# An adding DMA in a seven-product scheme: one weight sum moves from VectorE to a DMA, and ten groups get a fourth seven-product pair

## The chip, the cores and the metric

The kernel runs on one core of a Trainium2 chip. The metric is the time of one execution on the device in microseconds; runs of a kernel are compared by their medians.

## The reference

Two layers of a decoder trunk over 256 tokens of width 2048, in float32. Layer 0 mixes with sliding-window attention beside an mLSTM, layer 1 with forgetting attention; after each mixer stands a SwiGLU feed-forward part, and this is what the change touches:

```python
def swiglu(xn, w_gate, w_up, w_down):
    return (jax.nn.silu(xn @ w_gate) * (xn @ w_up)) @ w_down
...
h = h + swiglu(rms_norm(h, norm_ffn[layer]), w_gate[layer], w_up[layer], w_down[layer])
```

`w_gate` and `w_up` are 2048 x 5632, `w_down` is 5632 x 2048. The gain of the norm is put into the split activations (`xh`, `xl`), its scale `r` is applied after the products.

## The kernel before

Every float32 operand is split in two float32r parts, `hi` (a cast on ScalarE, lines 187 and 356) and `lo` (what is left, a subtraction on VectorE, lines 188 and 357), and a product is three matmuls (`three`, lines 532 to 534): hi x hi, hi x lo, lo x hi. The weights come from memory in tiles of 256 rows x 512 columns (512 KB, `load_raw`, line 134, issued by SP), and each tile's parts go into one of eight slots (`slot`, tiles `hi` and `lo`) that rotate: a slot is written again when TensorE has read what was in it.

A layer's 5632 hidden columns are eleven groups of 512. The groups come in three parts (0 to 2, 3 to 6, 7 to 10); behind each part stands the down product of its rows. `ffn` calls `pair_group` for each gate/up group, with the two weight matrices (gate columns, up columns), and for each pair of 512-column blocks of the down product. `pair_group` walks along the inner dimension in eight steps of 256 (six where a part has three groups), two row blocks of 128 at a time. Such a step is called a pair. With the two token blocks and the two matrices, a pair is a 2 x 2 by 2 x 2 block product, once for each column of 512. A *plain* pair does it in eight products, 24 matmuls, from two weight tiles split as they are. A *mixed* pair does it in seven products, 21 matmuls, in the manner of Strassen and Winograd: it needs sums of activation blocks (`sums`, made once and kept in `sx` and `sd`, `x4` for pair 7) and four sums of weight blocks, made for each pair on VectorE:

```python
ra, rb = (load_raw(w, k0, c0, NB, fp, W_RAWS if halves else RAWS, raws) for w, c0 in mats)
```

`ra` is the gate tile of the pair (rows k0, k0+1) and `rb` the up tile (for a down pair, the first and the second column block). Lines 607 to 610 make the four differences, 512 elements a partition each, into a tile `t4` and in place into `ra`; then `t4` and `ra` are split. `order` says which pairs are mixed: `ORDER` has three of eight, `HEAVY` four; a group takes `HEAVY` where its number is in `DENSE`, which is empty, so all groups take `ORDER`. At a group's end `combine` (lines 553 to 570) puts the products together, and silu and the product of gate and up follow (lines 665 to 672). Mixed pairs outside the feed-forward part take other buffers (`halves` given).

Raw tiles of mixed pairs rotate through `RAWS` = 4 buffers; a load waits until the tile four loads earlier was read for the last time. Raw tiles of plain pairs have four buffers of their own.

The program is written pair by pair, but a scheduler orders the instructions of each engine at build time. Each engine then works through its own queue in that order, and waits where an operand or a buffer is not ready. SP's queue holds the loads, GpSimd's the DMAs that it issues itself.

Of the kernel before, what the change touches and what calls it, by code (L numbers as in the profile page):

```python
# [7 lines left out]
F32 = mybir.dt.float32  # L8
# [4 lines left out]
ALU = mybir.AluOpType  # L13
# [4 lines left out]
P = 128  # L18
# [5 lines left out]
NB = 512  # L24
CK = 2
# [10 lines left out]
ORDER = ((0, 0), (1, 1), (0, 2), (1, 3), (0, 4), (1, 5), (0, 6), (0, 7))  # L36
HEAVY = ((1, 1), (0, 0), (1, 3), (0, 2), (1, 5), (0, 4), (1, 7), (0, 6))
FOURTH = 7
DENSE = ()
DOWN = {  # L40
    6: ((0, 0), (1, 1), (0, 2), (1, 3), (0, 4), (0, 5)),
    8: ((0, 0), (1, 1), (0, 2), (1, 3), (0, 4), (1, 5), (0, 6), (0, 7)),
# [9 lines left out]
W_RAWS = 4  # L52
LATER = (6, 10, 3, 5)
LATER_DOWN = (5, 6)
RAWS = 4
P_JOIN = 4
COLD = 9
TURNED = (0,)
# [17 lines left out]
def trunk(  # L76
# [19 lines left out]
    nc = tc.nc  # L96
# [31 lines left out]
    def load_raw(w, k0, c0, n, pool=wr, bufs=4, raws=None):  # L128
        if raws:
            raw = raws.pop(0)  # L130
            raws.append(raw)
        else:
            raw = pool.tile([P, CK, NB], F32, tag="raw", name="raw", bufs=bufs)
        loaded[0] = nc.sync.dma_start(
            raw[:, :, 0:n], w[k0 * P : (k0 + CK) * P, c0 : c0 + n].rearrange("(k p) n -> p k n", p=P)
        )
        return raw
# [46 lines left out]
    def split_chunk(raw, n):  # L184
        hi, lo = slot()
        for k in (slice(0, 1), slice(1, CK)) if any(raw is f for f in fine) else (slice(0, CK),):
            latest[0] = nc.scalar.copy(hi[:, k, 0:n], raw[:, k, 0:n])  # L187
            nc.vector.tensor_tensor(  # L188
                out=lo[:, k, 0:n], in0=raw[:, k, 0:n], in1=hi[:, k, 0:n].bitcast(F32), op=ALU.subtract
            )  # L190
        return hi, lo
# [71 lines left out]
    def sums_of(pool, sh, sl, copies, full=None, tags=("tmp", "tmp"), bufs=None, box=None, x4=None):  # L263
        if box is not None:
            full, s = box[:, 0:4, :].rearrange("p (i t) q -> p i t q", i=2), box[:, 4:8, :]
            copies(full.rearrange("p i t q -> p i (t q)"))
        elif full is None:
            full = pool.tile([P, 2, NT, P], F32, tag=tags[0], name="full", bufs=bufs)
            copies(full.rearrange("p i t q -> p i (t q)"))
        if box is None:  # L270
            s = pool.tile([P, 4, P], F32, tag=tags[1], name="s4", bufs=bufs)
        nc.vector.tensor_tensor(out=s[:, 0, :], in0=full[:, 0, 1, :], in1=full[:, 1, 1, :], op=ALU.add)
        nc.vector.tensor_tensor(out=s[:, 1, :], in0=s[:, 0, :], in1=full[:, 0, 0, :], op=ALU.subtract)
        nc.vector.tensor_tensor(out=s[:, 2, :], in0=full[:, 0, 0, :], in1=full[:, 0, 1, :], op=ALU.subtract)
        nc.vector.tensor_tensor(out=s[:, 3, :], in0=full[:, 1, 0, :], in1=s[:, 1, :], op=ALU.subtract)
        if x4 is None:
            split_plain(sh, sl, s)
        else:
            split_plain(sh, sl, s[:, 0:3, :])
            split_plain(x4[:, 0, :], x4[:, 1, :], s[:, 3, :])  # L280
# [258 lines left out]
    def pair_group(fp, par, lhs, sums, mats, order, todo=(), halves=None, inner=None, raws=None):  # L539
        plain = [[bank(par, "acc") for _ in range(NT)] for _ in range(2)]  # L540
        begun = set()

        def fresh(*at):
            known = at in begun
            begun.add(at)
            return not known

        todo = list(todo)
        prods = None
        kinds = [kind for kind, _ in order]  # L550
        t0, t1 = slice(0, P), slice(P, 2 * P)

        def combine(prods):
            c = fp.tile([P, 4, NB], F32, tag="c", name="c", bufs=1)
            nc.scalar.copy(c[:, 0, :], prods[0])
            if halves is None:
                nc.vector.tensor_tensor(out=c[:, 1, :], in0=prods[3], in1=c[:, 0, :], op=ALU.add)
                nc.vector.tensor_tensor(out=c[:, 2, :], in0=prods[2], in1=c[:, 1, :], op=ALU.add)
                nc.vector.tensor_tensor(
                    out=c[:, 1:4:2, :],  # L560
                    in0=prods[1].rearrange("p (a n) -> p a n", a=1).broadcast_to([P, 2, NB]),
                    in1=c[:, 1:3, :],
                    op=ALU.add,
                )
                return c
            nc.vector.tensor_tensor(out=c[:, 2, :], in0=prods[3], in1=c[:, 0, :], op=ALU.add)
            nc.vector.tensor_tensor(out=c[:, 1, :], in0=prods[2], in1=c[:, 2, :], op=ALU.add)
            nc.vector.tensor_tensor(out=c[:, 3, :], in0=prods[1], in1=c[:, 1, :], op=ALU.add)
            nc.vector.tensor_tensor(out=c[:, 2, :], in0=prods[1], in1=c[:, 2, :], op=ALU.add)
            return c  # L570

        for pos, (kind, pair) in enumerate(order):
            k0 = 2 * pair
            if inner is not None and pos == len(order) - 1:
                c = combine(prods)
                inner()
            if not kind:
                last = pos == len(order) - 1
                walk = [(i, t) for i in range(CK) for t in range(NT)]
                if last:  # L580
                    walk.sort(key=lambda it: it[1])
                for m, (w, c0) in enumerate(mats):
                    hi, lo = load_chunk(w, k0, c0, NB)
                    run_due(todo, pos)
                    for i, t in walk:
                        ah, al = lhs(k0 + i)
                        ts = slice(t * P, (t + 1) * P)
                        three(
                            plain[m][t], ah[:, ts], al[:, ts], hi[:, i, :], lo[:, i, :],
                            fresh(m, t), last and i == CK - 1,  # L590
                        )
                continue
            first, last = 1 not in kinds[:pos], 1 not in kinds[pos + 1 :]
            if first:
                prods = [bank(1 - par, "prod") for _ in range(4)]
            ra, rb = (load_raw(w, k0, c0, NB, fp, W_RAWS if halves else RAWS, raws) for w, c0 in mats)
            hg, lg = split_chunk(ra, NB)
            run_due(todo, pos)
            t4 = ra if halves else fp.tile([P, 2, NB], F32, tag="t4", name="t4", bufs=1)
            ta, tb, tc_, td = (  # L600
                (ra[:, 0, :], rb[:, 0, :], rb[:, 1, :], ra[:, 1, :])
                if halves
                else (t4[:, 0, :], t4[:, 1, :], ra[:, 0, :], ra[:, 1, :])
            )
            hu, lu = slot()
            split_plain(hu[:, 1, :], lu[:, 1, :], rb[:, 1, :])
            nc.vector.tensor_tensor(out=ta, in0=rb[:, 0, :], in1=ra[:, 0, :], op=ALU.subtract)
            nc.vector.tensor_tensor(out=tb, in0=rb[:, 1, :], in1=rb[:, 0, :], op=ALU.subtract)
            nc.vector.tensor_tensor(out=tc_, in0=rb[:, 1, :], in1=ta, op=ALU.subtract)
            nc.vector.tensor_tensor(out=td, in0=ra[:, 1, :], in1=tc_, op=ALU.subtract)  # L610
            parts = []
            for src in (ra, rb) if halves else (t4, ra):
                if halves:
                    hs, ls = halves.pop(0)
                    halves.append((hs, ls))
                else:
                    hs, ls = slot()
                split_plain(hs, ls, src)
                parts.append((hs, ls))
            where = ((0, 0), (1, 0), (1, 1), (0, 1)) if halves else ((0, 0), (0, 1), (1, 0), (1, 1))  # L620
            ht = [parts[a][0][:, b, :] for a, b in where]
            lt = [parts[a][1][:, b, :] for a, b in where]
            sh, sl = sums(pair)
            xa, la = lhs(k0)
            xb, lb = lhs(k0 + 1)
            three(prods[0], xa[:, t0], la[:, t0], hg[:, 0, :], lg[:, 0, :], first, last)
            three(plain[0][0], xb[:, t0], lb[:, t0], hg[:, 1, :], lg[:, 1, :], fresh(0, 0), False)
            three(plain[1][0], sh[3], sl[3], hu[:, 1, :], lu[:, 1, :], fresh(1, 0), False)
            three(prods[1], sh[0], sl[0], ht[0], lt[0], first, last)
            three(prods[2], sh[2], sl[2], ht[1], lt[1], first, last)  # L630
            three(prods[3], sh[1], sl[1], ht[2], lt[2], first, last)
            three(plain[0][1], xb[:, t1], lb[:, t1], ht[3], lt[3], fresh(0, 1), False)
        if inner is None:
            c = combine(prods)
        return plain, c
# [161 lines left out]
    with tc.tile_pool(name="ev", bufs=1) as ev:  # L797
# [223 lines left out]
        with tc.tile_pool(name="mp", bufs=1) as mp:  # L1021
# [8 lines left out]
            halves = spare_halves()  # L1030
# [123 lines left out]
    with tc.tile_pool(name="od", bufs=1) as od:  # L1154
# [12 lines left out]
        for t in range(NT):  # L1167
            nc.vector.scalar_tensor_tensor(
                out=fg[:, t, :],
# [207 lines left out]
```

## Time and profile before

| | |
|---|---|
| median of 3 runs | 2077.62 us (2076.95 to 2077.89) |
| profiled execution | 2077.56 us, its span 2075.9 us, granted clock 0.999 |
| PE, DVE, ACT, POOL busy | 2065.7, 1819.0, 1373.7, 44.6 us |
| DMA, share of 16 engines' span, queue of SP | 66.1%, 426.27 MB |
| matmuls, records in the trace | 9473 |

PE is TensorE, DVE VectorE, ACT ScalarE, POOL GpSimd. The feed-forward part of layer 0 runs from about 320 to 1010 us, that of layer 1 from about 1377 us to the end. The silu of line 667 marks the ends of the groups: in layer 0 at 365.4, 406.3, 447.1 us (the first part), 550.7, 592.9, 634.2, 675.2 us (the second), 799.6, 842.0, 883.4, 924.9 us (the third). Since instructions overlap within an engine, a duration is longer than the distance of two starts. In rows of idle time, the name behind the arrow is what ended it.

### The profile page before, as it was taken

Reading aid. Unit: us, or ns where it says so; the run is one execution under the profiler, and the core shown is the slowest. Engines: PE = TensorE matmul, PEld = TensorE weight load, DVE = VectorE, ACT = ScalarE, POOL = GpSimd, SP = SyncE. Lnnn points to the kernel's source line nnn. Section 1 sums busy time; section 2 is a strip of 40 time slices with the busy share of each in tenths; the row PEclk is TensorE's granted clock in tenths of the full one; section 3 lists DMA queues with packets and bytes.
Section 4 is the critical chain, followed back from the end, with each engine's and each line's share of the span. In section 5 each row is a group of like instructions: output and inputs, shape, how many; then the busy total and the mean of one; then the engine's idle time right before and its main releaser. Section 6 shows DMA issues by size and latency. Waiting matters only on the chain.

```text
span 2075.9 us, 26965 instructions
## 1 busy us (share of the span) xinstructions
PE 2065.7 (100%) x9473; PEld 1715.1 (83%) x9473; DVE 1819.0 (88%) x2367; ACT 1373.7 (66%) x1744; POOL 44.6 (2%) x66
## 2 busy tenths in 40 slices
PE   9999999999999999999999999999999999999998
PEld 7878888888888888888888888888888888888886
DVE  6788769999999999999899688689999999999994
ACT  6777678664676656667676776687655666556763
POOL 1010000000000000000000001000000000000000
PEclk9999999999999999999999999999999999999999
DMA  8566577666677666766676776586756677667764
GB/s 292 169 216 192 188 244 238 206 219 196 210 223 224 193 208 217 222 204 183 206 213 209 231 201 183 155 268 217 233 187 218 209 217 224 202 195 225 206 196 141
DMA packets 309576, 434.88 MB, mean 209 GB/s; under 512 B 106412, under 2 KB 114624, under 8 KB 309312
## 3 DMA queue, kind: packets, MB, share of 16 engines
q1 hardware_dynamic: 307088, 426.27, 66.1%
q0 software_dynamic: 1632, 5.80, 0.8%
q8 instruction: 74, 1.21, 0.2%
q10 hardware_dynamic: 720, 1.09, 0.2%
q14 instruction: 62, 0.51, 0.1%
HBM read 408.68 MB, written 2.12 MB: 198 GB/s over the span
## 4 chain that ended last, share of the span: by engine, by line
PE 97%; DVE 1%; ACT 1%; issue 1%; DMA 0%; POOLq 0%; POOL 0%; ACTq 0%; DVEq 0%
PE acc L532 21%; PE acc L534 21%; PE acc L533 21%; PE acc L223 6%; PE acc L222 6%; PE acc L224 6%; PE prod L532 5%; PE prod L533 5%; PE prod L534 5%; PE p L386 1%; PE po L487 1%; ACT s L420 0%; PE po L488 0%; DVE lo L188 0%; DMA raw<-in_w_down_dram 0%
## 5 line engine op out<-in xcount | busy, mean ns | idle before, releaser
L188 DVE TENSOR_TENSOR lo<-raw,hi 128x1024 fp32r<-128x1024 f32 (+3 forms) x656 | 771.1, 1195 | 135.5 <-ACT hi L187 133.0
L187 ACT CAST hi<-raw 128x1024 fp32r<-128x1024 f32 (+3 forms) x656 | 661.7, 1027 | 341.2 <-PE acc L534 137.2
L533 PE MATMUL acc<-lo,xh 128*128 128x512 f32 x1320 | 514.0, 389 | 0.0
L534 PE MATMUL acc<-hi,xl 128*128 128x512 f32 x1320 | 511.4, 389 | 0.0
L532 PE MATMUL acc<-hi,xh 128*128 128x512 f32 x1320 | 506.2, 390 | 0.0
L534 PEld LDWEIGHTS acc<-hi,xl 128*128 128x128 f32 x1320 | 247.8, 188 | 51.6
L533 PEld LDWEIGHTS acc<-lo,xh 128*128 128x128 f32 x1320 | 247.8, 188 | 51.4 <-issue 0.2
L532 PEld LDWEIGHTS acc<-hi,xh 128*128 128x128 f32 x1320 | 247.7, 188 | 51.3 <-issue 0.2
L356 ACT CAST hi<-raw 128x512 fp32r<-128x512 f32 x204 | 166.9, 819 | 160.7 <-PE acc L534 83.6
L357 DVE TENSOR_TENSOR lo<-raw,hi 128x512 fp32r<-128x512 f32 x204 | 191.6, 939 | 11.4 <-ACT hi L356 10.4
L533 PE MATMUL acc<-lo,mh 128*128 128x512 f32 x466 | 181.0, 389 | 0.0
L534 PE MATMUL acc<-hi,ml 128*128 128x512 f32 x466 | 180.3, 389 | 0.0
L532 PE MATMUL acc<-hi,mh 128*128 128x512 f32 x466 | 176.2, 389 | 0.1
L356 ACT CAST hi<-t 128x1024 fp32r<-128x1024 f32 x95 | 100.0, 1053 | 63.9 <-PE acc L534 38.0
L357 DVE TENSOR_TENSOR lo<-t,hi 128x1024 fp32r<-128x1024 f32 x95 | 116.2, 1224 | 15.2 <-ACT hi L356 15.0
L223 PE MATMUL acc<-lo,mh 128*128 128x512 f32 (+1 forms) x322 | 126.3, 392 | 0.0
L222 PE MATMUL acc<-hi,mh 128*128 128x512 f32 (+1 forms) x322 | 125.8, 391 | 0.0
L224 PE MATMUL acc<-hi,ml 128*128 128x512 f32 (+1 forms) x322 | 123.7, 391 | 0.0
L532 PEld LDWEIGHTS acc<-hi,mh 128*128 128x128 f32 x466 | 87.5, 188 | 18.5 <-ACT hi L187 0.5
L534 PEld LDWEIGHTS acc<-hi,ml 128*128 128x128 f32 x466 | 87.5, 188 | 18.2
L533 PEld LDWEIGHTS acc<-lo,mh 128*128 128x128 f32 x466 | 87.4, 188 | 18.2
L223 PE MATMUL acc<-lo,xh 128*128 128x512 f32 (+3 forms) x288 | 100.0, 348 | 0.2 <-DVE lo L188 0.2
(356 smaller groups left out, 3174.7 us busy)
## 6 DMA issues: line engine op xcount, KB each, us to landing
raw<-in_w_gate_dram SPq DMA_DIRECT2D x176, 512.0 KB, 4.5
raw<-in_w_up_dram SPq DMA_DIRECT2D x176, 512.0 KB, 4.6
raw<-in_w_down_dram SPq DMA_DIRECT2D x176, 512.0 KB, 4.8
raw<-in_w_in_odd_dram SPq DMA_DIRECT2D x88, 512.0 KB, 5.3
raw<-in_w_in_even_dram SPq DMA_DIRECT2D x51, 512.0 KB, 5.1
raw<-in_w_out_even_dram SPq DMA_DIRECT2D x32, 512.0 KB, 5.2
raw<-in_w_out_odd_dram SPq DMA_DIRECT2D x32, 512.0 KB, 4.7
hr<-in_w_in_even_dram SPq DMA_DIRECT2D x12, 512.0 KB, 4.5
```

What stands on the lines that cost most here:

```text
L187: latest[0] = nc.scalar.copy(hi[:, k, 0:n], raw[:, k, 0:n])
L188: nc.vector.tensor_tensor(out=lo[:, k, 0:n], in0=raw[:, k, 0:n], in1=hi[:, k, 0:n].bitcast(F32), op=ALU.subtract)
L222: nc.tensor.matmul(o, ah[:, ts], hi, start=(k == 0), stop=False)
L223: nc.tensor.matmul(o, ah[:, ts], lo, start=False, stop=False)
L224: nc.tensor.matmul(o, al[:, ts], hi, start=False, stop=(k == k_all - 1 and cs.stop == n))
L356: nc.scalar.copy(dst_h, src)
L357: nc.vector.tensor_tensor(out=dst_l, in0=src, in1=dst_h.bitcast(F32), op=ALU.subtract)
L386: nc.tensor.matmul(pq[j % 2][:, j // 2, :], q_of(j, b), k_of(j)[:, 0:cols], start=True, stop=True)
L487: nc.tensor.matmul(po, v_of(j, 0), tt[:, j, 0:2, :].rearrange("p c q -> p (c q)"), start=True, stop=False)
L532: nc.tensor.matmul(o, ah, hi, start=start, stop=False)
L533: nc.tensor.matmul(o, ah, lo, start=False, stop=False)
L534: nc.tensor.matmul(o, al, hi, start=False, stop=stop)
```

## The change

In the feed-forward part (`halves` is None) a mixed pair's weight sums are made another way. A DMA issued by GpSimd reads the first row block of the gate tile (128 x 512, 256 KB) from memory a second time and adds it onto the first row block of the up tile in its buffer, when that tile has landed. The sum is then in `rb` without VectorE; the whole of `rb` is split at once (before, its second half). One subtraction of 512 and one of 1024 elements, the latter with one operand read twice, take the place of four of 512. The signs of the activation sums and of the combination change with it. Tile `t4` is gone, and `RAWS` is 5. Five of the eleven gate/up groups, 1, 4, 5, 8 and 9, take `HEAVY`, with four mixed pairs. Elsewhere (`halves` given) only signs and the order of four operations change.

```diff
-DENSE = ()
+DENSE = (1, 4, 5, 8, 9)
...
-RAWS = 4
+RAWS = 5
...
-        nc.vector.tensor_tensor(out=s[:, 2, :], in0=full[:, 0, 0, :], in1=full[:, 0, 1, :], op=ALU.subtract)
+        nc.vector.tensor_tensor(out=s[:, 2, :], in0=full[:, 0, 1, :], in1=full[:, 0, 0, :], op=ALU.subtract)
...
                     in0=prods[1].rearrange("p (a n) -> p a n", a=1).broadcast_to([P, 2, NB]),
                     in1=c[:, 1:3, :],
-                    op=ALU.add,
+                    op=ALU.subtract,
...
             ra, rb = (load_raw(w, k0, c0, NB, fp, W_RAWS if halves else RAWS, raws) for w, c0 in mats)
+            if halves is None:
+                (w, c0), part = mats[0], slice(k0 * P, (k0 + 1) * P)
+                nc.gpsimd.dma_start(rb[:, 0, :], w[part, c0 : c0 + NB], accum_op=ALU.add)
             hg, lg = split_chunk(ra, NB)
             run_due(todo, pos)
-            t4 = ra if halves else fp.tile([P, 2, NB], F32, tag="t4", name="t4", bufs=1)
-            ta, tb, tc_, td = (
-                (ra[:, 0, :], rb[:, 0, :], rb[:, 1, :], ra[:, 1, :])
-                if halves
-                else (t4[:, 0, :], t4[:, 1, :], ra[:, 0, :], ra[:, 1, :])
-            )
             hu, lu = slot()
-            split_plain(hu[:, 1, :], lu[:, 1, :], rb[:, 1, :])
-            nc.vector.tensor_tensor(out=ta, in0=rb[:, 0, :], in1=ra[:, 0, :], op=ALU.subtract)
-            nc.vector.tensor_tensor(out=tb, in0=rb[:, 1, :], in1=rb[:, 0, :], op=ALU.subtract)
-            nc.vector.tensor_tensor(out=tc_, in0=rb[:, 1, :], in1=ta, op=ALU.subtract)
-            nc.vector.tensor_tensor(out=td, in0=ra[:, 1, :], in1=tc_, op=ALU.subtract)
...
+            if halves is None:
+                split_plain(hu, lu, rb)
+                nc.vector.tensor_tensor(out=rb[:, 1, :], in0=rb[:, 0, :], in1=rb[:, 1, :], op=ALU.subtract)
+                both = rb[:, 1, :].rearrange("p (a n) -> p a n", a=1).broadcast_to([P, CK, NB])
+                nc.vector.tensor_tensor(out=ra, in0=ra, in1=both, op=ALU.subtract)
+                hc, lc = (a[:, 0, :] for a in slot())
+                split_plain(hc, lc, rb[:, 1, :])
+                hd, ld = slot()
+                split_plain(hd, ld, ra)
+                ht = [hu[:, 0, :], hd[:, 0, :], hc, hd[:, 1, :]]
+                lt = [lu[:, 0, :], ld[:, 0, :], lc, ld[:, 1, :]]
```

In the changed file the adding DMA is line 599, the new subtractions are lines 605 and 607, and what stood at 665 and 669 stands at 671 and 675.

GpSimd's queue in the changed kernel, from the end of layer 0's mixer on (`r` is the scaling of the norm):

```order
L1108 TENSOR_TENSOR st<-st,mhalf 128x2 x4
L599 DMA raw<-in_w_gate_dram 128x512 x3
L254 TENSOR_TENSOR r<-tot,mhalf 128x2
L599 DMA raw<-in_w_gate_dram 128x512 x7
L599 DMA raw<-in_w_down_dram 128x512 x4
L599 DMA raw<-in_w_gate_dram 128x512 x14
L599 DMA raw<-in_w_down_dram 128x512 x6
```

The queue holds 54 adding DMAs in layer 0 and 51 in layer 1; before, only `r` stood there.

VectorE's queue in the second gate/up group of layer 0, before, with two of its mixed pairs (tiles `raw_3570`, `raw_3572` and `raw_3640`, `raw_3642`, gate and up):

```order
L188 TENSOR_TENSOR lo_3103<-raw_3640,hi_3102 128x1024
L610 TENSOR_TENSOR raw_3570<-raw_3570 128x512
L607 TENSOR_TENSOR t4_3646<-raw_3642,raw_3640 128x512
L608 TENSOR_TENSOR t4_3646<-raw_3642 128x512
L188 TENSOR_TENSOR lo_3099<-raw_3608,hi_3098 128x1024
L609 TENSOR_TENSOR raw_3640<-raw_3642,t4_3646 128x512
L188 TENSOR_TENSOR lo_3101<-raw_3624,hi_3100 128x1024
L357 TENSOR_TENSOR lo1_3097<-raw_3570,hi1_3096 128x1024
L610 TENSOR_TENSOR raw_3640<-raw_3640 128x512
L357 TENSOR_TENSOR lo_3105<-raw_3642,hi_3104 128x512
L357 TENSOR_TENSOR lo_3107<-t4_3646,hi_3106 128x1024
```

And in the same group now, from the last use of the first mixed pair's gate tile `raw_3462` to the first use of the third one's up tile `raw_3600`, which is loaded into the buffer of `raw_3462`:

```order
L357 TENSOR_TENSOR lo1_3097<-raw_3462,hi1_3096 128x1024
L671 TENSOR_TENSOR c_3433<-acc_3116,c_3433 128x512
L671 TENSOR_TENSOR c_3433<-acc_3117,c_3433 128x512
L671 TENSOR_TENSOR c_3433<-acc_3118,c_3433 128x512
L357 TENSOR_TENSOR lo_3107<-raw_3532,hi_3106 128x512
L607 TENSOR_TENSOR raw_3530<-raw_3530,raw_3532 128x1024
L675 TENSOR_SCALAR c_3433<-c_3433,r_3113 128x512
L357 TENSOR_TENSOR lo_3101<-raw_3600,hi_3100 128x1024
```

The four differences and the half split of the up tile have become the whole split of it and two subtractions. Six rows stand between a release and a use that a load and an adding DMA separate.

The same queue now in the third group, from the last use of its first mixed pair's gate tile `raw_3806` to the first use of the third one's up tile `raw_3944`:

```order
L357 TENSOR_TENSOR lo_3101<-raw_3806,hi_3100 128x1024
L675 TENSOR_SCALAR c_3745<-c_3745,r_3113 128x512
L357 TENSOR_TENSOR lo_3109<-raw_3876,hi_3108 128x1024
L675 TENSOR_SCALAR c_3745<-c_3745,r_3113 128x512
L605 TENSOR_TENSOR raw_3876<-raw_3876 128x512
L357 TENSOR_TENSOR lo_3105<-raw_3944,hi_3104 128x1024
```

Four rows stand between here. In the first group of the part and in most later places it is twice to five times as much work.

More of the change, by code (lines that the diff above doesn't have):

```diff
@@ L567, in combine @@
             nc.vector.tensor_tensor(out=c[:, 1, :], in0=prods[2], in1=c[:, 2, :], op=ALU.add)
-            nc.vector.tensor_tensor(out=c[:, 3, :], in0=prods[1], in1=c[:, 1, :], op=ALU.add)
-            nc.vector.tensor_tensor(out=c[:, 2, :], in0=prods[1], in1=c[:, 2, :], op=ALU.add)
+            nc.vector.tensor_tensor(out=c[:, 3, :], in0=prods[1], in1=c[:, 1, :], op=ALU.subtract)
+            nc.vector.tensor_tensor(out=c[:, 2, :], in0=prods[1], in1=c[:, 2, :], op=ALU.subtract)
             return c
@@ L605, in pair_group @@
-            hu, lu = slot()
-            split_plain(hu[:, 1, :], lu[:, 1, :], rb[:, 1, :])
-            nc.vector.tensor_tensor(out=ta, in0=rb[:, 0, :], in1=ra[:, 0, :], op=ALU.subtract)
-            nc.vector.tensor_tensor(out=tb, in0=rb[:, 1, :], in1=rb[:, 0, :], op=ALU.subtract)
-            nc.vector.tensor_tensor(out=tc_, in0=rb[:, 1, :], in1=ta, op=ALU.subtract)
-            nc.vector.tensor_tensor(out=td, in0=ra[:, 1, :], in1=tc_, op=ALU.subtract)
-            parts = []
-            for src in (ra, rb) if halves else (t4, ra):
-                if halves:
+            hu, lu = slot()
@@ new lines, in pair_group @@
+            if halves is None:
[9 more added lines that the diff above has]
+                lt = [lu[:, 0, :], ld[:, 0, :], lc, ld[:, 1, :]]
+            else:
+                split_plain(hu[:, 1, :], lu[:, 1, :], rb[:, 1, :])
+                nc.vector.tensor_tensor(out=ra[:, 0, :], in0=rb[:, 0, :], in1=ra[:, 0, :], op=ALU.add)
+                nc.vector.tensor_tensor(out=rb[:, 0, :], in0=rb[:, 1, :], in1=rb[:, 0, :], op=ALU.subtract)
+                nc.vector.tensor_tensor(out=rb[:, 1, :], in0=ra[:, 0, :], in1=rb[:, 1, :], op=ALU.subtract)
+                nc.vector.tensor_tensor(out=ra[:, 1, :], in0=ra[:, 1, :], in1=rb[:, 1, :], op=ALU.subtract)
+                parts = []
+                for src in (ra, rb):
@@ L614, in pair_group @@
                     hs, ls = halves.pop(0)
                     halves.append((hs, ls))
[L616 to L622, printed above, removed]
+                    split_plain(hs, ls, src)
+                    parts.append((hs, ls))
@@ L623, in pair_group @@
+                where = ((0, 0), (1, 0), (1, 1), (0, 1))
+                ht = [parts[a][0][:, b, :] for a, b in where]
+                lt = [parts[a][1][:, b, :] for a, b in where]
             sh, sl = sums(pair)
```

## The prediction

> **What bounds the kernel now.** I read the page first, its busy times and its chain of waits.
>
> ```profile
> PE 2065.7 (100%) x9473; PEld 1715.1 (83%) x9473; DVE 1819.0 (88%) x2367; ACT 1373.7 (66%) x1744; POOL 44.6 (2%) x66
> ...
> PE 97%; DVE 1%; ACT 1%; issue 1%; DMA 0%; POOLq 0%; POOL 0%; ACTq 0%; DVEq 0%
> ```
>
> TensorE is busy for the whole span and 97% of the chain is on it. What one matmul costs is its cadence, not its duration, since matmuls overlap. The timeline of PE in the feed-forward part shows it (first and last of ten rows):
>
> ```profile
> 849.83 0.39 PE L534 MATMUL acc<-hi,sx 128*128 128x512 f32 x1
> ...
> 851.87 0.39 PE L534 MATMUL prod<-hi,sx 128*128 128x512 f32 x1
> ```
>
> Nine steps in 2.04 us are 0.227 us for a 512-column matmul. Only fewer matmuls, or a stall, can move the time by much. Next, how much room VectorE leaves: the windows of the first three gate/up groups of layer 0 (columns: us, PE, PEld, DVE, ACT, POOL busy, clock, DMA share, GB/s).
>
> ```profile
> 324.50:365.40 40.90, 40.90 (x182) 33.88 (x181) 37.25 (x56) 34.74 (x49) 0.69 (x1) 1.00 0.76 227
> 365.40:406.30 40.90, 40.90 (x183) 33.84 (x182) 39.08 (x50) 28.18 (x32) 0.00 (x0) 1.00 0.65 208
> 406.30:447.10 40.80, 40.80 (x182) 33.78 (x181) 40.47 (x51) 29.18 (x32) 0.00 (x0) 1.00 0.72 230
> ```
>
> VectorE idles 3.65, 1.82 and 0.33 us in them. So TensorE is the bound, with VectorE right behind it. Just after the third group the chain in order of time leaves TensorE for once:
>
> ```profile
> 459.47 0.23 PE acc L532
> 459.75 0.48 issue
> 460.23 1.06 ACT hi L187
> 461.32 1.24 DVE lo L188
> 462.57 5.61 DMA raw<-in_w_down_dram
> 468.25 0.92 issue
> 469.16 1.05 ACT hi L187
> 470.26 0.50 PE acc L532
> ```
>
> TensorE here takes a split chunk as soon as it exists: a buffer is released by VectorE, loaded (5.61 us), cast, used. The lead of the split work is used up at that point, in the kernel as it is. A later operand in this stretch of a layer is a later end.
>
> **The change part by part.** *Matmuls removed.* A mixed pair takes seven products of three matmuls, a plain pair eight. Ten groups (five in each of two layers) get one more mixed pair: 10 x 3 = 30 matmuls x 0.227 = 6.8 us. TensorE was gapless there, so all of it is on the path if nothing is late.
>
> *VectorE work.* Its cadences, from the timeline (start to start: 0.60 us for 512 elements, 1.13 us for 1024), with the group of a 1024-element operation that reads one operand broadcast, as the new subtraction does:
>
> ```profile
> 425.65 0.69 DVE L357 TENSOR_TENSOR lo<-raw,hi 128x512 fp32r<-128x512 f32 x1
> 426.25 1.22 DVE L357 TENSOR_TENSOR lo<-t,hi 128x1024 fp32r<-128x1024 f32 x1
> 427.38 0.69 DVE L609 TENSOR_TENSOR raw<-raw,t 128x512 f32<-128x512 f32 x1
> ```
>
> ```profile
> L559 DVE TENSOR_TENSOR c<-prod,c 128x1024 f32<-128x1024 f32 x33 | 40.4, 1223 | 0.0
> ```
>
> A mixed pair had three operations of 1024 and five of 512: 6.4 us. It now has four and two: 5.7 us. A plain pair has two of 1024: 2.3 us. A group with three mixed pairs gets 3 x 0.67 = 2.0 us lighter; a dense one goes from 3 x 6.4 + 5 x 2.3 = 30.7 to 4 x 5.7 + 4 x 2.3 = 32.0 (unrounded 1.5 us more). The second group would hold 39.08 + 1.5 = 40.6 us of VectorE work against 40.9 - 0.7 = 40.2 us of matmuls. ScalarE casts the same number of elements in a mixed pair as before. It has room on average, but it works in order.
>
> *The adding DMA.* One for each mixed pair of gate, up and down: 105, 256 KB each, from GpSimd's queue. GpSimd is all but idle; the scaling by the norm, L254 there, now stands behind the first three and is needed only at that group's end. What matters is a new link in a chain: buffer free, load, **add**, cast of the up tile, lo part. Rows for the links:
>
> ```profile
> raw<-in_w_up_dram SPq DMA_DIRECT2D x176, 512.0 KB, 4.6
> ...
> raw<-in_w_in_even_dram SPq DMA_DIRECT2D x10, 256.0 KB, 2.9
> ...
> h<-in_x_dram POOLq DMA_DIRECT2D x4, 512.0 KB, 6.9
> cb<-scratch POOLq DMA_DIRECT2D x4, 512.0 KB, 6.2
> ...
> rows<-mt POOLq DMA_DIRECT2D x1, 4.0 KB, 1.7
> ```
>
> ```profile
> L356 ACT CAST hi<-t 128x1024 fp32r<-128x1024 f32 x95 | 100.0, 1053 | 63.9 <-PE acc L534 38.0 <-PE prod L534 13.1 <-DVE lo L357 7.6
> ```
>
> No row shows an adding DMA. From below it is a 4 KB transfer of GpSimd's queue, 1.7 us; from above a 512 KB one that queues behind its like, 6.9 us (it reads and writes 256 KB at the destination besides reading 256 KB from memory). I take 4.0: nearest is the 256 KB row, 2.9, and the queue's 512 KB row is 1.6 longer than SP's, of which I count two thirds. Chain C = 4.6 + 4.0 + 1.05 = 9.7 us (bounds 7.4 and 12.6).
>
> The Trainium skill, page "DMA: Bandwidth & Descriptors", section "Anatomy of one DMA — SWDGE (gpsimd) path", fits a fixed 2.0 us plus bytes over 436e3 per microsecond for this queue. For 256 KB that is an estimate of 2.6 us, with which the sum below would end at 2079; the trace's 512 KB rows are 3 us above that fit, so I go by the rows.
>
> *Where the chain isn't covered.* With five raw buffers, the up tile of a mixed pair is loaded into the gate buffer of the pair two before, free only after that pair's last lo part; with four, it took the up buffer of the pair two before, free earlier. In the new order of VectorE the work between that release and the first use of the sum is mostly 11 to 20 us, above C. But in the second group the second, third and fourth mixed pair have 4.8, 4.1 and 6.9 us between, and the last of the third group 2.9 us (the 4.1: five of 512 and one of 1024, 3.0 + 1.13; the 2.9: three of 512 and one of 1024, 1.8 + 1.13). Both layers have the same order. VectorE and ScalarE work in order, so what is queued behind the waiting cast and its lo part, other pairs' splits among it, waits too, and TensorE waits for that. VectorE's delays: after two places 2 x 9.7 - 8.9 = 10.5 us; after four 4 x 9.7 - 18.7 = 20.1 us.
>
> Cover: the idle time of the first group and what its three pairs give back, 3.65 + 2.0 = 5.7 us. The second group adds nothing (1.82 - 1.5 - 0.7 = -0.4), the third 0.33 + 2.0, so 7.6 us at the fourth place. TensorE then loses 4.8 us by the second place and 12.5 by the fourth. I take the middle, 8.7 us a layer, since the idle time of today is itself partly waiting that the new waits replace. Later groups and the down parts have more work in between, and I count them at nothing; if they are not covered, each uncovered microsecond of a pair is added.
>
> *Sum.* 2 x 8.7 - 6.8 = +10.5 us. The profiled execution took 2077.56 us, its span being 2075.9, and the median is 2077.62: the forecast is **2088**. With C at 7.4 the same middle gives 1.8 us a layer and 2074; with 12.6 it gives 17.4 and 2106.
>
> **Rivals.** *The sum arrives in time* (faster). All 30 matmuls are then won: 2077.6 - 6.8 = 2070.8. For it: TensorE shows no gap today although ScalarE waits for loads:
>
> ```profile
> ACT hi L187 <- DMA raw<-in_w_down_dram: 30.8, 25, 3.8
> ```
>
> So split work can wait 3.8 us without harm, and VectorE gets lighter in 12 of 22 groups. Against it: those waits are for down weights, and the places above are in the gate/up groups with the least idle time. It decides where C is under 7.3 us (two places need 2C = 8.9 + 5.7), or where the lead is some 6 us larger than I count.
>
> *VectorE becomes the bound, no DMA is late* (no change). A dense group then lasts its 40.6 us of VectorE work in place of 40.9: 10 x 0.3 = 3 us won, 2074.6. For it: VectorE's share of 96 to 99% in these windows. Against it: the lighter groups beside the dense ones build up lead.
>
> *The change doesn't do what it says.* The new order holds 30 fewer 128x512 matmuls and the 105 adding DMAs, so I give this no chance.
>
> **How the numbers follow.** A measurement of this kernel can tell about 0.2%, 4.2 us, from no change. Late sums, as forecast: 0.58, of which 0.04 falls within 0.2% (C near 8 us); VectorE as the bound: 0.06, within; sums in time: 0.36, faster. So faster 0.36, same 0.10, slower 0.54. The slower case alone has a range of 2080 to 2106. The other sign holds more than 0.2, so the range reaches down to 2070.5, just under the full gain, and up to 2106, the bound with the slowest row.
>
> **What would show it.** Right: idle time of TensorE between 365 and 475 us and again some 1057 us later, several microseconds in all, ended by VectorE's lo parts and ScalarE's casts, and these by the adding DMA; its landing near 4 us; later dense groups 0.7 us shorter than today. The cadence stays 0.227 us. Wrong: a TensorE as gapless as today (then the lead or the load was better than I count), a landing under 2.5 us, or waits in the later dense groups, which would put the loss on VectorE's load and not on the chain.

## The result, and the profile after

The changed kernel took **2097.21 us** (median of 4 runs, 2095.33 to 2098.77), the kernel before 2077.76 (4 runs, 2076.95 to 2078.23): a ratio of 1.0094, 95% interval 1.0076 to 1.0111. It is slower by 0.9%, on the side that the prediction called likeliest and inside its range, 9.2 us above its value. The profiled execution took 2095.33 us, its span 2093.6, 17.7 us more than before.

The same lines of the page, after (busy times, GpSimd's queue, the chain of waits):

```profile
PE 2072.1 (99%) x9443; PEld 1709.8 (82%) x9443; DVE 1794.4 (86%) x2217; ACT 1384.1 (66%) x1764; POOL 133.7 (6%) x171
...
q0 software_dynamic: 16752, 33.33, 9.0%
...
PE 75%; DVE 8%; DMA 6%; ACT 5%; issue 4%; SPq 0%; ACTq 0%; POOLq 0%; POOL 0%; DVEq 0%
```

The 30 matmuls are gone (9473 to 9443) and VectorE has 24.6 us less to do, yet TensorE's share of the chain fell from 97% to 75%: the rest of the chain runs over VectorE, transfers and casts. (A share of the chain is not time lost: TensorE is busy for 99% of the span.) The page's DMA rows price the transfers (KB each, median us from issue to landing):

```profile
raw<-in_w_gate_dram SPq DMA_DIRECT2D x176, 512.0 KB, 5.2
raw<-in_w_up_dram SPq DMA_DIRECT2D x176, 512.0 KB, 5.4
raw<-in_w_down_dram SPq DMA_DIRECT2D x176, 512.0 KB, 5.7
...
raw<-in_w_gate_dram POOLq DMA_DIRECT2D x76, 256.0 KB, 5.7
...
raw<-in_w_down_dram POOLq DMA_DIRECT2D x29, 256.0 KB, 6.8
```

In the median the adding DMA lands in 5.7 us, in the down parts in 6.8; the forecast had 4.0. The up tile's load, 4.6 before, takes 5.4. The chain in order of time, in layer 0's third group (start, us, what), goes through the very link that was forecast:

```profile
417.46 0.61 DVE lo L357
418.07 0.02 issue
418.09 4.70 DMA raw<-in_w_up_dram
...
422.86 0.55 issue
423.41 4.69 DMA raw<-in_w_gate_dram
...
428.25 1.06 ACT hi L356
429.31 0.02 issue
429.33 1.23 DVE lo L357
```

VectorE's last lo part frees the buffer at 418.07, the up tile is loaded, the gate block is added, ScalarE casts, and VectorE goes on at 429.33: 11.3 us. ScalarE's waits say the same (us in total, times, longest; the cast of line 356 takes, among others, the up tile with the sum in it):

```profile
ACT hi L356 <- DMA raw<-in_w_gate_dram: 27.4, 9, 5.8
```

The windows (columns as in the prediction) show the first three groups of layer 0 and, in the fourth row, the next part of that layer, groups 4 to 7; the last row is the same part before:

```profile
324.50:368.20 43.70, 42.88 (x185) 33.96 (x184) 33.77 (x51) 34.28 (x49) 3.28 (x4) 1.00 0.78 214
368.20:413.50 45.30, 42.92 (x177) 33.74 (x176) 41.58 (x49) 30.85 (x36) 3.43 (x4) 0.96 0.80 230
413.50:456.70 43.20, 42.06 (x182) 33.62 (x181) 37.94 (x45) 27.70 (x32) 2.56 (x3) 1.00 0.75 219
...
560.00:807.50 247.50, 247.50 (x1094) 205.01 (x1093) 229.12 (x250) 158.17 (x175) 17.07 (x20) 1.00 0.79 234
```

```profile
550.70:799.60 248.90, 248.90 (x1100) 206.10 (x1099) 234.02 (x278) 156.30 (x171) 0.00 (x0) 1.00 0.67 211
```

In the second group 177 matmuls take 45.3 us; before, 183 took 40.9. In the later part TensorE has no idle time, and six matmuls fewer make it 1.4 us shorter, 0.23 us each: there the change does what it is for, although 20 adding DMAs run beside it.

All of TensorE's lost time follows from the starts of its matmuls: for every start that comes more than 0.25 us after the one before, what exceeds 0.227 us, summed by place (us). "Groups 1, 2, 3" are the first three gate/up groups of a layer, "down" the 45 to 60 us behind them. Each row is from one profiled execution.

| kernel | layer 0: groups 1, 2, 3, down | layer 1: the same | all of the program |
|---|---|---|---|
| before | 0.0, 0.0, 0.0, 0.6 | 0.0, 0.0, 0.0, 0.2 | 11.5 |
| after | 2.1, 5.6, 2.3, 0.7 | 2.9, 4.5, 4.5, 0.6 | 35.8 |
| up_first | 2.3, 0.0, 0.0, 1.0 | 2.9, 0.0, 0.0, 1.0 | 19.2 |
| no_dense | 2.6, 0.0, 0.0, 0.9 | 3.5, 0.0, 0.0, 0.2 | 20.5 |
| plain_copy | 0.8, 2.2, 1.7, 1.8 | 2.4, 2.5, 1.9, 1.4 | 26.6 |
| up_v0 | 0.2, 0.0, 0.3, 1.3 | 0.3, 0.3, 0.4, 0.4 | 16.8 |

After minus before is 24.3 us, of which 22.4 stand at these places. With 30 x 0.227 = 6.8 us won, that makes 17.5; the spans differ by 17.7.

### The profile page after: what moved, and what is told of

Same layout as the page of the kernel before. It is cut to its first block, busy times and chain, and to the rows that moved or that the text cites. A ratio compares the mean times of both kernels' runs of the same rounds, so it can differ in the third digit from the quotient of the medians.

```text
span 2093.6 us, 27094 instructions
## 1 busy us (share of the span) xinstructions
PE 2072.1 (99%) x9443; PEld 1709.8 (82%) x9443; DVE 1794.4 (86%) x2217; ACT 1384.1 (66%) x1764; POOL 133.7 (6%) x171
## 3 DMA queue, kind: packets, MB, share of 16 engines
q0 software_dynamic: 16752, 33.33, 9.0%
## 4 chain that ended last, share of the span: by engine, by line
PE 75%; DVE 8%; DMA 6%; ACT 5%; issue 4%; SPq 0%; ACTq 0%; POOLq 0%; POOL 0%; DVEq 0%
PE acc L533 16%; PE acc L532 16%; PE acc L534 16%; PE prod L533 4%; PE prod L532 4%; PE prod L534 4%; PE acc L222 4%; PE acc L223 4%; PE acc L224 4%; DVE lo L188 2%; DVE lo L357 2%; DMA raw<-in_w_down_dram 2%; ACT hi L187 2%; DMA raw<-in_w_gate_dram 1%; ACT hi L356 1%
## 5 line engine op out<-in xcount | busy, mean ns | idle before, releaser
L188 DVE TENSOR_TENSOR lo<-raw,hi 128x1024 fp32r<-128x1024 f32 (+2 forms) x646 | 761.7, 1194 | 153.8 <-ACT hi L187 151.2
L187 ACT CAST hi<-raw 128x1024 fp32r<-128x1024 f32 (+2 forms) x646 | 651.6, 1026 | 319.8 <-PE acc L534 83.7
L533 PE MATMUL acc<-lo,xh 128*128 128x512 f32 x1260 | 491.7, 391 | 1.0 <-DVE lo L188 1.0
L534 PE MATMUL acc<-hi,xl 128*128 128x512 f32 x1260 | 490.1, 390 | 0.0
L532 PE MATMUL acc<-hi,xh 128*128 128x512 f32 x1260 | 478.6, 392 | 5.5 <-ACT hi L187 3.9
L356 ACT CAST hi<-raw 128x1024 fp32r<-128x1024 f32 (+1 forms) x329 | 291.4, 894 | 226.5 <-DVE raw L605 84.6
L357 DVE TENSOR_TENSOR lo<-raw,hi 128x1024 fp32r<-128x1024 f32 (+1 forms) x329 | 334.9, 1029 | 52.2 <-ACT hi L356 50.8
L533 PEld LDWEIGHTS acc<-lo,xh 128*128 128x128 f32 x1260 | 236.8, 188 | 53.0 <-DVE lo L188 3.9
L607 DVE TENSOR_TENSOR raw<-raw 128x1024 f32<-128x1024 f32 x105 | 128.3, 1222 | 1.0
L599 POOL DMA_DIRECT2D raw<-in_w_gate_dram x76 | 65.1, 856 | 963.9 <-DMA raw<-in_w_up_dram 391.4
```

The costliest lines, as they stand in the source:

```text
L188: nc.vector.tensor_tensor(out=lo[:, k, 0:n], in0=raw[:, k, 0:n], in1=hi[:, k, 0:n].bitcast(F32), op=ALU.subtract)
L356: nc.scalar.copy(dst_h, src)
L357: nc.vector.tensor_tensor(out=dst_l, in0=src, in1=dst_h.bitcast(F32), op=ALU.subtract)
L532: nc.tensor.matmul(o, ah, hi, start=start, stop=False)
L533: nc.tensor.matmul(o, ah, lo, start=False, stop=False)
L534: nc.tensor.matmul(o, al, hi, start=False, stop=stop)
```

## The experiments

Each was compared with runs of the kernel before on its own chip (medians 2077.16 to 2078.02). The theory is that of the prediction: late sums, by the chain from a free buffer over the load and the adding DMA to the cast. Every edit also lets the scheduler order the queues of all engines anew, so what is compared are whole kernels.

**up_first.** The order of the two loads of a feed-forward mixed pair is turned, nothing else:

```diff
-            ra, rb = (load_raw(w, k0, c0, NB, fp, W_RAWS if halves else RAWS, raws) for w, c0 in mats)
+            if halves is None:
+                rb, ra = (load_raw(w, k0, c0, NB, fp, RAWS, raws) for w, c0 in mats[::-1])
+            else:
+                ra, rb = (load_raw(w, k0, c0, NB, fp, W_RAWS, raws) for w, c0 in mats)
```

> One line: of each feed-forward mixed pair the up tile is loaded before the gate tile, so with five buffers the up tile takes the gate buffer of the pair three before (not two before), and the gate tile the up buffer of the pair two before. In VectorE's new order no adding DMA has under 12 us of VectorE work between the release of its buffer and the first use of its sum (before this edit: 4.8, 4.1, 6.9 and 2.9 us at four places of a layer). Same matmuls, same adding DMAs, same VectorE work. Theory (the chain release, load, add, cast, some 12 us, is uncovered at those places): the stalls between 340 and 480 us and 1057 us later go, all 30 matmuls are won, 2071 us, at most 2075. Rival, VectorE is the bound in the dense groups: the stalls stay, 2090 to 2098. Rival, the added traffic slows all loads: they stay too, 2090 to 2098.

2079.67 us (11 runs), ratio to before 1.0007 (0.9998 to 1.0016): 17.5 us of the loss are back, though the 2075 that the theory allowed at most is missed. The adding DMAs are as many, and those of gate and up land as late as in the changed kernel (those of the down parts in 5.7 us in place of 6.8):

```profile
raw<-in_w_gate_dram POOLq DMA_DIRECT2D x76, 256.0 KB, 5.7
```

And the dense second group passes in 38.40 us without idle time of TensorE (windows, groups 1 and 2 of layer 0):

```profile
324.50:370.60 46.10, 45.29 (x195) 35.76 (x193) 41.29 (x59) 38.09 (x53) 3.31 (x4) 1.00 0.84 232
370.60:409.00 38.40, 38.40 (x171) 31.81 (x170) 35.40 (x41) 28.41 (x34) 3.10 (x4) 1.00 0.78 244
```

ScalarE's casts of line 356 wait for no adding DMA any more; the row of 27.4 us has no counterpart. So neither the adding DMA as such nor VectorE's load made the second and third group late, but the point at which the up tile's load could start. The edit moves two things there, the buffer that the up tile takes and its place ahead of the gate tile in SP's queue, and does not tell them apart; the changed kernel with four or six raw buffers, which would move the buffer alone, was not run. The full gain would have been 2071: 8 us stay lost, 5.2 of them in the first groups of the two layers. There the chain in order of time runs through another transfer:

```profile
343.67 0.69 DVE lo L357
344.37 0.02 issue
344.38 4.56 DMA raw<-in_w_gate_dram
348.94 0.03 issue
...
349.13 1.22 DVE raw L610
```

Now the gate tile, which is loaded second, waits for a buffer that VectorE frees at 344.37, and its subtraction waits for its landing. The loads of this group also stand behind eight transposing DMAs in SP's queue (timeline of up_first):

```profile
324.08 10.38 SPq L317 DMA_TRANSPOSE box<-box  x8
```

**no_dense.** The changed kernel with the adding DMAs, but with three mixed pairs in every group:

```diff
-DENSE = (1, 4, 5, 8, 9)
+DENSE = ()
```

> The changed kernel with three mixed pairs in every group, so the adding DMAs (95) without the extra pairs; matmuls as in the kernel before. Its order of VectorE has two adds of a layer with short cover, 5.2 and 6.3 us, in place of four. Theory (chain): 2 x 12.2 - 11.5 = 13 us of delay a layer less some 8 us of cover, 5 us a layer: 2088, between 2080 and 2094. Rival, VectorE is the bound in the dense groups: VectorE is lighter than before in every group and nothing is lost, 2078. Rival, added traffic: a tenth fewer adds, so nearly the whole loss stays beside the 6.8 us of matmuls, 2100.

2087.14 us (4 runs), 1.0047 (1.0034 to 1.0061). There is a loss without a dense group, 9 us with all 9473 matmuls, and the theory's 2088 is met, but by luck: it had 5 us a layer at two late sums, and in the table groups 2 and 3 have no gap, while the first groups have 2.6 and 3.5 (the rest lies between the parts and the layers). The late sums of groups 2 and 3 thus need the fourth mixed pair; that it does so by bringing the pairs closer together is argued, not shown. The first group's loss does not need it.

**dense_dve.** The kernel before, with its sums on VectorE, and the five dense groups:

```diff
-DENSE = ()
+DENSE = (1, 4, 5, 8, 9)
```

> The kernel before with four mixed pairs in the same five groups: the extra pairs alone, all sums still on VectorE, no adding DMA. A dense group then has 39.1 + 4.1 = 43.2 us of VectorE work against 40.2 us of matmuls. Theory: VectorE becomes the bound there, each of the ten dense groups is up to 2.3 us longer than today, less the lead of the groups beside them: 2088 to 2101, with TensorE waiting all through the dense groups and not at single places. If it stays under 2078, VectorE's load doesn't decide and the adding DMA has no work to take away.

2092.69 us (4 runs), 1.0073 (1.0059 to 1.0087). Windows of its groups 2 and 6 of layer 0:

```profile
367.10:411.80 44.70, 43.17 (x188) 34.77 (x187) 44.55 (x57) 31.20 (x34) 0.00 (x0) 1.00 0.70 215
596.40:644.70 48.30, 45.32 (x197) 36.34 (x196) 46.06 (x58) 31.42 (x35) 0.00 (x0) 1.00 0.65 206
```

VectorE is busy for 44.55 of 44.70 us, and TensorE waits. Summed as in the table, groups 2, 6 and 10 lose 2.3, 3.9 and 1.7 us in layer 0 and 2.7, 3.0 and 1.7 in layer 1, in gaps of up to 2.1 us and not all through, as was expected; groups 5 and 9, the first of two dense ones in a row, lose nothing. The longest gap, 3.1 us, stands at 994 us, behind the last group. A dense group does need the sums taken off VectorE; in the changed kernel the dense groups after the first part run without a gap (the row from 560.00 on above), but for 0.7 us in group 10 of layer 0.

**plain_copy.** GpSimd's DMA copies and does not add (what is left out is the addition, so the products are others):

```diff
-                nc.gpsimd.dma_start(rb[:, 0, :], w[part, c0 : c0 + NB], accum_op=ALU.add)
+                nc.gpsimd.dma_start(rb[:, 0, :], w[part, c0 : c0 + NB])
```

> The changed kernel with the DMA on GpSimd's queue as a plain load of the same 256 KB into the same place, without adding (the sums are left out, so the products are not the reference's). It prices the adding itself: beside 5.7 us (gate) and 6.8 us (down) to landing. If the add makes the transfer slow, it lands at about 4 us, C is 1.5 to 2 us less, and at the four places a layer the kernel gains 3 to 4 times that: 2082 to 2088. If it is the queue and the issue that cost, it lands near 5.5 us and the time stays at 2095.

2085.6 us (4 runs), 1.0036 (1.0022 to 1.0049), against 1.0094 with the addition. Its page:

```profile
q0 software_dynamic: 10032, 33.33, 4.9%
...
raw<-in_w_gate_dram POOLq DMA_DIRECT2D x76, 256.0 KB, 4.8
```

The DMA lands 0.9 us earlier, the up tile's load 0.3 us (5.1), and 11.6 us are back, 9.2 us between the two profiled executions. Eight late places with 1.2 us less each make 9.6: the places take the transfer's time several times over, as a chain without cover does. It is not the landing alone that differs: the DMA engines also have less to do (4.9% against 9.0%), and the slow matmuls of the last section, 2.4 us, are absent.

**up_v0, up_d0, v012**, and **up_v0_d10** ask where up_first's 8 us went. In up_v0 VectorE makes the sums again in the first group of each layer, in place (`vec`), and the up tile is loaded first elsewhere:

```diff
+BY_VECTOR = (0,)
...
+            if halves is None and not vec:
+                rb, ra = (load_raw(w, k0, c0, NB, fp, RAWS, raws) for w, c0 in mats[::-1])
...
+                    vec=g in BY_VECTOR,
```

> The up tile is loaded first in all groups that add by DMA, and in the first gate/up group of each layer VectorE makes all the weight sums again (four subtractions or additions of 512 in place, no adding DMA); dense groups as in the changed kernel, 30 matmuls fewer. Theory A: what up_first still lost (8 us against the full gain) is the first group alone, where the loads stand behind eight transposing DMAs in SP's queue and the adding DMA comes 6 us behind the late load; then the gaps of TensorE near 350 and 1410 us are gone and the time is 2071 to 2073. Theory B: the loss there is VectorE's own work at a place where it is short; with 0.7 us more for each pair the gaps stay or grow, 2078 to 2081.

2075.21 us (11 runs), 0.9985 (0.9976 to 0.9994): the fastest of all kernels here, by 0.15%; the interval leaves out 1, but it is less than the 0.2% that the prediction took for its bound. The gaps of the first groups are gone (0.2 and 0.3 in the table), as theory A said, though this does not single out the adding DMA, since other work of the group is reordered too; the time is 2 us above its range, since the first down part of layer 0 (1.3) and the stretch between the layers have grown. Its chain is on TensorE again for 93%:

```profile
PE 93%; DVE 3%; DMA 2%; issue 1%; ACT 1%; SPq 0%; POOLq 0%; POOL 0%; DVEq 0%; ACTq 0%
```

up_d0 is up_first with `DENSE = ()`.

> The up tile first as in up_first, but no group has four mixed pairs: 9473 matmuls as before. Theory A: what up_first lost lies in the first group of a layer, which isn't dense; the gaps near 350 and 1410 us stay, and the time is before's plus some 7 us, 2084 to 2086. Theory B: the loss came from the dense groups' VectorE work; without them no gap and before's time, 2077 to 2079.

2080.91 us (10 runs), 1.0017 (1.0007 to 1.0026): between the two theories, 3 us above before. Its gaps in the first groups are 0.5 and 2.1, where up_first had 2.3 and 2.9. So with this order of loads the first group's loss depends in part on the dense group behind it, which neither theory had; with the changed kernel's order (no_dense) it did not.

v012 keeps the changed kernel's order of loads and gives VectorE the sums of groups 1 to 3 (`BY_VECTOR = (0, 1, 2)`), with four dense groups (`DENSE = (4, 5, 8, 9)`).

> The loads in the order of the changed kernel (gate tile first); in the first three gate/up groups of each layer VectorE makes the weight sums, without an adding DMA; from the fourth group on, and in the down parts, the adding DMA stays. Dense are 4, 5, 8, 9: 24 matmuls fewer, 5.4 us. Theory A: the loss of the changed kernel lies at its late sums in the first part of a layer alone; without them no gap between 340 and 480 us, 2072 to 2074. Theory B: the adding DMAs late in the layer also cost something (their traffic, the down parts); 2077 or more.

2081.55 us (10 runs), 1.0017 (1.0008 to 1.0026): theory A missed by 8 us, theory B's 2077 or more holds. Its gaps are in the first down parts, 4.5 and 2.2 us, where adding DMAs still stood, and 1.2 and 1.6 us in the second group of layer 0 and the first of layer 1.

up_v0_d10 is up_v0 with ten dense groups, 60 matmuls fewer than before.

> As up_v0, but all groups except the first of a layer have four mixed pairs: 60 matmuls fewer than before, 13.6 us. Theory A: adding DMAs leave VectorE enough room, and nothing else is late: 2064 to 2066. Theory B: with ten dense groups VectorE's 40.6 us a group are the bound over TensorE's 40.2, or its queue makes casts late: the last ten dense groups win nothing, 2071 to 2076.

2085.4 us (5 runs, 2081.91 to 2088.99), 1.0038 (1.0025 to 1.005): both theories missed, the slower by 9 us. In the profiled execution, the fastest of the five, the gaps come to 28.3 us in all, before's 11.5 among them, and lie scattered: 4.5 us between 420 and 480 us, 2.8 between 960 and 1020, 3.3 between 1680 and 1740. What ended each was not followed up.

**v012d** and **up_v0_dn** take the adding DMA out of the first down part of v012 and of up_v0:

```diff
-                    fp, 1 - n0 // 2, m_of, sums_d, [(wd, n0 * NB), (wd, (n0 + 1) * NB)], order, todo
+                    fp, 1 - n0 // 2, m_of, sums_d, [(wd, n0 * NB), (wd, (n0 + 1) * NB)], order, todo,
+                    vec=g0 == 0,
```

> As v012 (gate tile first, VectorE's sums in the first three groups, dense 4, 5, 8, 9, 24 matmuls fewer), and VectorE makes the sums of the first down part too, so that no adding DMA stands before the fourth group. Theory A: v012 lost its 8 us to late sums of the first down part (the gaps at 467 and 1528 us) and to the first pairs of the second group; without the former 2075 to 2077. Theory B: all that is left is lost elsewhere, by VectorE's order or slower loads: 2080 to 2083 as v012.

> As up_v0 (up tile first, VectorE's sums in the first group of a layer, five dense groups), and VectorE also makes the sums of the first down part of each layer, where up_v0 still waited for a down tile at 468 us. Theory A: the remaining loss (up_v0 stands 4 us above the full gain) is partly there: 2072 to 2074. Theory B: TensorE waits there for a plain load and VectorE's queue, not for the adding DMA; 2075 to 2077.

v012d took 2076.63 us (10 runs), 0.9995 (0.9986 to 1.0004), as theory A had it: the gaps of the down parts fell from 4.5 and 2.2 to 1.8 and 1.1. With the changed kernel's own order of loads, and the adding DMAs kept to where they have cover, the kernel is as fast as before; but most of the 5.4 us that its 24 matmuls are worth is still lost, since its gaps come to 17.0 us, 5.5 more than before's. up_v0_dn took 2077.92 (11 runs), 1.0000 (0.9991 to 1.0009), 2.7 us slower than up_v0 and above both theories' ranges: with VectorE's sums in the down part the gap there grew to 4.0 us in layer 0, 1.6 us of it eight slow matmuls (last section). In up_v0's own chain the adding DMA was not what was late there: from 462.74 us it runs over a plain down load (4.86 us) to the cast of line 188, which takes tiles as they were loaded.

**idle_add** and **no_add** measure the traffic by itself. In both VectorE makes all sums in place (`BY_VECTOR = range(11)`, also in the down parts), with four raw buffers and no dense group. idle_add issues the adding DMAs all the same, onto tiles that nobody reads; they are 95 (66 of gate and 29 of down), and not the 105 that were expected, since no group is dense:

```diff
+                spare = spares[fp].pop(0)
+                spares[fp].append(spare)
+                nc.gpsimd.tensor_copy(spare[:, 0:8], rb[:, 0, 0:8])
+                nc.gpsimd.dma_start(spare, w[part, c0 : c0 + NB], accum_op=ALU.add)
```

> The 105 adding DMAs without their place in the chain: VectorE makes all weight sums in place (four operations of 512 for a pair), no dense groups, four raw buffers; for each mixed pair GpSimd still issues an adding DMA of the same 256 KB of the same matrix, once the up tile has landed, onto one of two spare tiles that nobody reads. Theory A: the loss is the link between load and use, not the traffic: 2078 to 2081, no gaps between 340 and 480 us, though the loads may land later than before (4.6 us). Theory B: the traffic itself and the slower loads cost: 2085 or more.

> The control of idle_add: the same in-place sums on VectorE, no dense groups, four raw buffers, and no adding DMA at all; idle_add ran 2087.5. Theory A: the adding DMAs' traffic cost idle_add nothing that counts; its loss is that the in-place sums hold the up tile's buffer until its last split, where before a tile of its own took two sums; then 2085 to 2088. Theory B: the traffic of the 105 DMAs and the loads that land later cost idle_add its 10 us; then before's time, 2077 to 2079, with loads back at 4.5 to 4.8 us.

idle_add took 2087.53 us (4 runs), 1.0047 (1.0033 to 1.0061), which alone would have spoken for the traffic, as its theory B. Its control no_add took 2086.02 (5 runs), 1.0043 (1.003 to 1.0057): no difference that can be told. The loads do land later with the traffic, no_add's rows first:

```profile
raw<-in_w_up_dram SPq DMA_DIRECT2D x176, 512.0 KB, 5.0
raw<-in_w_down_dram SPq DMA_DIRECT2D x176, 512.0 KB, 5.2
```

```profile
raw<-in_w_up_dram SPq DMA_DIRECT2D x176, 512.0 KB, 5.5
raw<-in_w_down_dram SPq DMA_DIRECT2D x176, 512.0 KB, 5.6
...
spare<-in_w_gate_dram POOLq DMA_DIRECT2D x66, 256.0 KB, 5.6
```

The traffic adds 0.4 to 0.5 us a load. The medians of the two kernels differ by 1.5 us, where nothing waits for the sum; by the two intervals a cost of up to some 5 us is not excluded. The 9 us that both lose are those of sums in place. My reason for them, a buffer held until its last split, is not shown: the largest gap, before 990 us, stands behind VectorE's sums for two pairs, one operation after the other (chain of no_add; L617 to L620 are the four operations of a pair):

```profile
980.09 0.60 DVE raw L618
980.69 0.60 DVE raw L617
981.29 0.60 DVE raw L619
981.89 0.60 DVE raw L618
982.49 0.60 DVE raw L620
983.10 0.60 DVE raw L619
```

The same weakness may sit in the groups that v012, v012d, up_v0 and up_v0_dn gave back to VectorE, so those four are bounds for what the adding DMA costs there, and no exact prices.

## Why the prediction was right, point by point

*The matmuls.* 30 fewer, and where nothing is late they are won: 1.4 us for six in the later part of layer 0, against 6 x 0.227 = 1.4.

*VectorE.* 24.6 us less in all; the prediction's terms make it 28 (12 groups x 2.0 and 29 down pairs x 0.67 less, 10 dense groups x 1.5 more). up_first, with the same work on VectorE, has no gap in a dense group. The rival of VectorE as the bound falls for this kernel; it is what stopped the dense groups in dense_dve.

*The link.* Shown: the chain of after goes through it, turning two loads takes away all the gaps of groups 2 and 3 (5.6 + 2.3 + 4.5 + 4.5 = 16.9 us), and with a copy in place of the adding DMA, landing 0.9 us sooner, 11.6 of the 19.5 us are back.

*The landing*, the term that was mis-sized. C was taken as 4.6 + 4.0 + 1.05 = 9.7. The medians of all transfers would make it 5.4 + 5.7 + 1.05 = 12.2, but what counts are the eight places that the prediction named, four a layer. There the trace has the up tile's load at 3.6 to 5.6 us (mean 4.3), then 0.6 to 0.8 us until the adding DMA starts, which the sum did not have, the DMA at 4.2 to 6.2 us (mean 4.9), and from the load's issue to the end of the cast 9.3 to 12.0 us, 11.0 in the mean. Two thirds of a queue's surcharge was too little: the addition costs 0.9 us over the copy, and the copy of 256 KB takes 4.8 where SP's row of that size has 2.9. The Trainium skill's fit for this queue ("DMA: Bandwidth & Descriptors", section "Anatomy of one DMA — SWDGE (gpsimd) path"), which gave an estimate of 2.6 us, does not hold for either: 4.8 for the copy and 5.7 with the addition, beside a load on other queues. But the prediction's "the trace's 512 KB rows are 3 us above that fit" left out a third such row, a single DMA into `dt__1241` that took 3.8 us before, 0.6 above it; so the rows that it went by were the slow ones of that queue.

*The cover.* With C at 11.0 the prediction's own sum would give 7.4 us after two places, 17.7 after four, the middle 12.5 a layer, and 2096. Measured in the second and third group and the down part were 8.0 us in layer 0 and 9.4 in layer 1 above before: 17.4, just the 2 x 8.7 of the forecast. That this is so exact is luck: a chain taken too short and a middle of two bounds taken too high cancelled, and 2.4 of the 17.4 are slow matmuls (last section) that the sum did not have.

*The place.* The 8.0 us of layer 0 lie in the stretch named, the 9.4 of layer 1 some 1057 to 1068 us later. But the first group, which I had counted as cover for its 3.65 us of idle VectorE, lost 2.1 and 2.9 us itself: with the 2.2 us of the next paragraph and the 1.9 us by which the profiled execution was faster than the median, that makes up the 9.2 us by which the forecast fell short. The adding DMA is not on the chain there. In layer 0 it runs over ScalarE, which waited 1.46 us for a transposing DMA at 331.5 us and then worked without a pause until the matmul at 352.86 us:

```profile
342.72 2.37 ACT hi L356 x3
345.09 1.61 ACT xh L361 x4
...
350.30 1.04 ACT hi L187
...
352.86 0.74 PE acc L532 x2
```

In layer 1 it runs over VectorE's lo parts and sums. Why these queues are later there than before is not shown.

*The later groups at nothing.* Nearly so: 0.8 us in layer 0's second and third part, none in layer 1's. The rest, 1.4 us, came between the layers.

## What to carry to other kernels

An operation handed to a DMA adds its landing to a chain, and what decided here is when the destination's load can start, not how idle the queue is: loading first the tile that gets the extra step took 17.5 of 19.5 us back. Look for the places where a buffer's release and the next use lie close together, and leave those to the engine that did the work before, which has its own price (up_v0_dn). A control without the suspected cost is worth its run: idle_add alone would have put the blame on the traffic.

## What was not expected of the hardware

An adding DMA takes the DMA engines twice the time of a copy. In the rows of GpSimd's queue the 105 DMAs take 16752 - 1632 = 15120 packets, 144 each, against 10032 - 1632 = 8400, 80 each, for the copy; and 8.2% of 16 engines' span (2093.6 us), 26 us of one engine for each, against 4.1% (of 2084.4), 13 us.

Short stalls cost a second time. Windows of after behind its two densest clusters of gaps (the eighth column is the granted clock):

```profile
383.50:387.50 4.00, 3.88 (x10) 3.10 (x11) 4.00 (x5) 4.00 (x6) 0.49 (x1) 0.57 0.60 84
...
1501.00:1503.50 2.50, 2.50 (x6) 1.82 (x6) 2.50 (x4) 2.50 (x4) 0.00 (x0) 0.50 0.47 94
```

```profile
383.98 0.63 PE L532 MATMUL acc<-hi,xh 128*128 128x512 f32 x1
384.41 0.63 PE L533 MATMUL prod<-lo,sx 128*128 128x512 f32 x1
384.83 0.63 PE L534 MATMUL prod<-hi,sx 128*128 128x512 f32 x1
```

The matmuls start 0.43 us apart in place of 0.227 for eight and for four steps, some 2.4 of the 24.3 us lost. v012 and up_v0_dn have eight such steps each, at 471 and 467 us, in their grown gaps, dense_dve six at 995 us, behind its gap of 3.1 us; up_first and up_v0 have no such series. The Trainium skill, page "TensorE: Matmul & The Clock Gate", section "Part 1: The HAM clock gate", has the clock halved after an idle window of about 3.4 us. The half rate agrees; but in the changed kernel no single gap of TensorE was longer than 1.1 us: several short ones within 4 to 5 us came before the half rate (TensorE was busy for 2.25 of the 3.50 us from 380.00 us on).
